# Holding back the third load of a row-gradient kernel until its first store is issued

## The chip, the cores and the metric

The kernel runs on one core of one Trainium2 chip. Its time is the device time of one execution in microseconds (us). A profile is one further execution, recorded by the hardware profiler; its span runs from the first to the last instruction, and its own device time is a little longer than its span.

## The reference

The input is an 8192 x 8192 array of float32, 268.4 MB. The output has the same size and is the gradient along each row:

```python
def reference(x: np.ndarray) -> np.ndarray:
    return np.gradient(x, axis=1)
```

Inside a row each output is half the difference of the right and the left neighbour. The first output of a row is the second element minus the first, the last one is the last element minus the one before it. There is one subtraction and one product for each element, and all 268.4 MB have to be read and 268.4 MB written: 536.9 MB through the core's 16 DMA engines.

## The kernel before

The rows are cut into 32 sets (`nsets`) of 256 rows. Each of the 128 partitions takes two whole rows (`R = 2`), which is 16384 elements, so a set is a tile of 128 x 16384 float32, 8.39 MB. Three buffers in SBUF, `slot0` to `slot2` (`NB = 3`), hold the sets in turn: set i lives in slot i mod 3. A slot has 64 elements of room in front of the input (`SH = 64`), and the result is written over the input, shifted to the left by that room.

One set goes through these steps. The line numbers are those of the profile.

1. The load (line 66) is one DMA of 8.39 MB. It is issued from SyncE's queue, shown as SP and, among the DMA queues, as q1. The load of set i + 3 waits for the store of set i, because it reuses its slot. It is queued right after set i's own work (line 120).
2. GpSimd (POOL) computes the differences at the ends of each row into `ends` (line 77). This is the first reader of the load, and so its start marks the landing of the load.
3. VectorE (DVE) computes the inner differences, halved, in one custom instruction of 128 x 16382 elements (line 88).
4. DVE, or in 12 sets POOL, copies the row ends into the result (line 99).
5. In sets 1 to 29 TensorE (PE) does two matmuls of 128 x 512 on zeros, whose result nobody reads (line 107). They wait for step 4, and the store waits for them. They serve as a pause.
6. The store (line 112) is one DMA of 8.39 MB from ScalarE's queue, shown as ACT and, among the DMA queues, as q10. The last two sets store from SP's queue, and the last set is computed and stored in two halves.

The work is in program order on every engine; `tc.manual_schedule()` leaves the order as written, and `chain` and `follow` name the instructions that each step has to wait for. At the start the loads of sets 0, 1 and 2 are issued one after the other, without any wait (line 71). They are moved in this order, since they are on one queue. The store of set 0 has no pause before it (`if 0 < i < nsets - 2`, line 103).

A DMA of 8.39 MB is split over all 16 DMA engines. Its packets are 64 KB each, 8 for each engine. The profile counts 5040 packets on q1 and 4320 on q10, the small writes that signal completion among them.

Of the kernel before, what the change touches and what calls it, by code (L numbers as in the profile page):

```python
# [1 line left out]

# [4 lines left out]


@with_exitstack
def kernel(  # L10
    ctx: ExitStack,
    tc: tile.TileContext,
    x: bass.AP,
    out: bass.AP,
):

    nc = tc.nc
    P = nc.NUM_PARTITIONS
    n, m = x.shape
    R = 2
    NB = 3
    SH = 64  # L30
    W = R * m
    nsets = n // (P * R)
    f32 = x.dtype

    x_sets = x.rearrange("(s p t) m -> s p (t m)", p=P, t=R)
    out_sets = out.rearrange("(s p t) m -> s p (t m)", p=P, t=R)

    pool = ctx.enter_context(tc.tile_pool(name="pool", bufs=1))
    slots = [pool.tile([P, SH + W], f32, name=f"slot{k}", tag=f"slot{k}") for k in range(NB)]
    ends = pool.tile([P, nsets, R, 2], f32, name="ends", tag="ends")  # L40
    zeros = pool.tile([P, 512], f32, name="zeros", tag="zeros")
    psum = ctx.enter_context(tc.tile_pool(name="psum", bufs=1, space=bass.MemoryType.PSUM))
    unread = psum.tile([1, 512], f32, name="unread", tag="unread")
    loads, stores = [], [[] for _ in range(nsets)]
    in_front = {}

    def chain(i, ins, *needed):

        group, engine = f"slot{i % NB}", ins.ins.engine
        keep = [o.ins for o in needed]
        if in_front.get(engine, (None,))[0] == group:
            keep.append(in_front[engine][1])
        tc.declare_no_dep(ins.ins, group=group, keep=keep, reason="implied by the needed step")
        tc.add_to_no_dep_group(group, ins.ins)
        in_front[engine] = group, ins.ins
        return ins

    def follow(ins, needed, reason):  # L60
        edge = mybir.DependencyInfo(mybir.DependencyClass.Sync, mybir.DependencyReason.DATA)
        tc.add_manual_dep(ins.ins, needed.ins.name, edge, reason=reason)

    def load(i):
        b = slots[i % NB]
        ins = nc.sync.dma_start(out=b[:, SH : SH + W], in_=x_sets[i])  # L66
        loads.append(chain(i, ins, *(stores[i - NB] if i >= NB else [])))

    with tc.manual_schedule():
        nc.vector.memset(zeros[:], 0.0)  # L70
        for i in range(NB):
            load(i)
        for i in range(nsets):
            b = slots[i % NB]
            xin = b[:, SH : SH + W].rearrange("p (t m) -> p t m", m=m)

            ins = nc.gpsimd.tensor_sub(  # L77
                out=ends[:, i, :, :],
                in0=xin[:, :, 1 : m : m - 2],
                in1=xin[:, :, 0 : m - 1 : m - 2],  # L80
            )
            at = [chain(i, ins, loads[i])]
            last = i == nsets - 1
            nr = 1 if last else R
            for r in range(0, R, nr):
                c0, c1 = r * m + 1, (r + nr) * m - 1

                ins = nc.vector._custom_dve(  # L88
                    dve_ops.TENSOR_TENSOR_REDUCE_SUB_MAX,
                    out=b[:, c0:c1],  # L90
                    in0=b[:, SH + c0 + 1 : SH + c1 + 1],
                    in1=b[:, SH + c0 - 1 : SH + c1 - 1],
                    s0=0.0,
                    s1=0.5,
                )
                halved = chain(i, ins, *at)
                res = b[:, r * m : (r + nr) * m].rearrange("p (t m) -> p t m", m=m)
                placer = nc.gpsimd if i % 5 in (1, 3) and not last else nc.vector
                ins = placer.tensor_copy(out=res[:, :, 0 : m : m - 1], in_=ends[:, i, r : r + nr, :])  # L99
                placed = chain(i, ins, halved)  # L100
                queue = nc.scalar if i < nsets - 2 else nc.sync
                pause = None
                if 0 < i < nsets - 2:


                    for k in range(2):
                        pause = nc.tensor.matmul(  # L107
                            out=unread[:], lhsT=zeros[:, 0:1], rhs=zeros[:], start=True, stop=True
                        )
                        if k == 0:  # L110
                            follow(pause, placed, "after the tile is computed")
                ins = queue.dma_start(  # L112
                    out=out_sets[i, :, r * m : (r + nr) * m], in_=b[:, r * m : (r + nr) * m]
                )
                stores[i].append(chain(i, ins, placed))
                if pause:
                    follow(ins, pause, "after the pause")
                at = [halved]
            if i + NB < nsets:
                load(i + NB)  # L120


# [1 line left out]
_INS = ['x']  # L124
_OUTS = [((8192, 8192), 'float32')]


# [23 lines left out]
```

## Time and profile before

| | us |
|---|---|
| six executions | 1248.38, 1248.56, 1248.81, 1257.55, 1257.81, 1261.25 |
| their median | 1253.18 |
| the profiled execution's own time | 1262.37 |
| its span | 1259.4 |
| DVE busy | 555.3 (44% of the span) |
| PE busy | 102.2 (8%) |
| POOL busy | 8.9 (1%) |
| packets on q1 and q10, share of 16 engines' span | 52.5% and 46.6% |

The six executions fall into two groups, one at 1248.4 to 1248.8 us and one at 1257.6 to 1261.3 us, with nothing between them; the median lies in the gap. The profiled execution is 1.1 us above the highest of the six.

Times inside the profile are us from the start of the span. Engine rows of the page show the busy share in tenths for 40 slices of the span, 31.5 us each. A row of the timeline gives the start, the duration, the engine, the line and the operation; the bracket at its end gives how long the engine had been idle and what it had waited for. Rows that end in "x3" or "x5" merge several instructions, and their duration runs from the first start to the last end. A row of the windows gives a stretch, the busy time of each engine in it, the granted TensorE clock, and last the DMA engines' mean busy share and the GB/s of the packets that started in it.

### The profile page before, as it was taken

To read this page: it belongs to the slowest core of one execution; us is meant where nothing else is said; L and a number is where in the kernel's file an instruction comes from. 1 tells how busy PE (TensorE), PEld (TensorE's weight loads), DVE (VectorE), ACT (ScalarE), POOL (GpSimd) and SP (SyncE) were. 2 spreads that over 40 slices of the span, in tenths; PEclk is the share of its full clock that TensorE was granted. 3 is DMA by queue.
4 is the path that set the end of the run, shared out by engine and by line. 5 is a ranking of instruction groups with operands and counts; after the bars stand their busy time and mean duration, and the time that the engine had idled before them with its cause. 6 is when DMAs were issued, how large, how long until landed. Compare 5 with 4: busy or idle time off the path is not lost.

```text
span 1259.4 us, 501 instructions
## 1 busy us (share of the span) xinstructions
PE 102.2 (8%) x116; PEld 9.8 (1%) x116; DVE 555.3 (44%) x55; POOL 8.9 (1%) x48
## 2 busy tenths in 40 slices
PE   0001110111100111011110111101111001110000
PEld 0000000000000000000000000000000000000000
DVE  2841555235553245523555335553345532455343
POOL 0000000000000000000000000000000000000000
PEclk9999995555555555555555555555555555555555
DMA  9999999999999999999999999999999999999996
GB/s 406 427 433 433 431 433 433 431 435 435 435 439 433 441 433 439 431 433 431 433 433 423 416 433 433 433 433 431 431 406 431 439 427 433 418 414 433 433 433 275
DMA packets 9361, 536.89 MB, mean 426 GB/s; under 512 B 1040, under 2 KB 1040, under 8 KB 1040
## 3 DMA queue, kind: packets, MB, share of 16 engines
q1 hardware_dynamic: 5040, 285.21, 52.5%
q10 hardware_dynamic: 4320, 251.66, 46.6%
q8 instruction: 1, 0.02, 0.0%
HBM read 268.44 MB, written 268.44 MB: 426 GB/s over the span
## 4 chain that ended last, share of the span: by engine, by line
DMA 70%; DVE 14%; another core or an unknown queue 9%; issue 3%; PE 2%; POOL 0%; SPq 0%; POOLq 0%; ACTq 0%
DMA slot<-in_x_dram 36%; DMA out_dram<-slot 34%; DVE slot L88 14%; PE unread L107 2%; POOL ends L77 0%; DVE slot L99 0%; SPq L66 0%; POOL slot L99 0%; POOLq L146 0%; ACTq L112 0%
## 5 line engine op out<-in xcount | busy, mean ns | idle before, releaser
L88 DVE CUSTOM_DVE_ANT_0 slot<-slot 128x16382 f32<-128x16382 f32 (+1 forms) x33 | 551.3, 16707 | 680.7 <-POOL ends L77 680.7
L107 PE MATMUL unread<-zeros 128*1 128x512 f32 x116 | 102.2, 1035 | 1065.4 <-DVE slot L99 603.9
L107 PEld LDWEIGHTS unread<-zeros 128*1 128x1 f32 x116 | 9.8, 104 | 1156.0 <-DVE slot L99 633.1
L77 POOL TENSOR_TENSOR ends<-slot 128x4 f32<-128x4 f32 x32 | 6.4, 200 | 1002.9 <-DMA slot<-in_x_dram 1002.9
L99 DVE COPY slot<-ends 128x4 f32<-128x4 f32 (+1 forms) x21 | 3.6, 172 | 0.7
L99 POOL COPY slot<-ends 128x4 f32<-128x4 f32 x12 | 2.3, 192 | 207.9 <-DVE slot L88 207.9
L70 DVE MEMSET zeros<- 128x512 f32 x1 | 0.5, 485 | 0.9 <-PEq L135 0.9
L135 POOL MEMSET const-bfloat16-1.0<- 128x1 bf16 x1 | 0.1, 103 | 0.0
L135 POOL MEMSET const-uint8-127<- 128x1 uint8 x1 | 0.1, 103 | 0.0
L135 POOL MEMSET const-float32-0.0<- 128x1 f32 x1 | 0.1, 99 | 0.2 <-issue 0.2
L135 POOL MEMSET const-float32-1.0<- 128x1 f32 x1 | 0.1, 99 | 0.0
## 6 DMA issues: line engine op xcount, KB each, us to landing
out_dram<-slot SPq DMA_DIRECT2D x2, 4096.0 KB, 20.3
slot<-in_x_dram SPq DMA_DIRECT2D x32, 48.9
out_dram<-slot ACTq DMA_DIRECT2D x30, 47.6
out_dram<-slot SPq DMA_DIRECT2D x1, 35.9
```

The costliest lines, as they stand in the source:

```text
L70: nc.vector.memset(zeros[:], 0.0)
L77: ins = nc.gpsimd.tensor_sub(out=ends[:, i, :, :], in0=xin[:, :, 1 : m : m - 2], in1=xin[:, :, 0 : m - 1 : m - 2],)
L88: ins = nc.vector._custom_dve(dve_ops.TENSOR_TENSOR_REDUCE_SUB_MAX, out=b[:, c0:c1], in0=b[:, SH + c0 + 1 : SH + c1 + 1], in1=b[:, SH + c0 ...
L99: ins = placer.tensor_copy(out=res[:, :, 0 : m : m - 1], in_=ends[:, i, r : r + nr, :])
L107: pause = nc.tensor.matmul(out=unread[:], lhsT=zeros[:, 0:1], rhs=zeros[:], start=True, stop=True)
L135: nc = _bacc.Bacc("TRN2", target_bir_lowering=False, num_devices=1)
```

## The change

Four things are different. The loads of sets 0 and 1 alone are issued at the start. The load of set 2 is issued from SP after the pause of set 0, the same pause that the store of set 0 now waits for; so that store and that load are released together. The pause of set 0 is new and short: one matmul of 128 columns. And ACT's queue, which the stores use, begins with a load of 16 x 16 elements into a small tile `few` that nobody reads.

```diff
     zeros = pool.tile([P, 512], f32, name="zeros", tag="zeros")
+    few = pool.tile([16, 16], f32, name="few", tag="few")
...
         nc.vector.memset(zeros[:], 0.0)
-        for i in range(NB):
-            load(i)
+
+        nc.scalar.dma_start(out=few[:], in_=x[0:16, 0:16])
+        load(0)
+        load(1)
         for i in range(nsets):
...
                 pause = None
-                if 0 < i < nsets - 2:
+                if i < nsets - 2:


-                    for k in range(2):
+                    for k in range(2 if i else 1):
+                        c = 512 if i else 128
                         pause = nc.tensor.matmul(
-                            out=unread[:], lhsT=zeros[:, 0:1], rhs=zeros[:], start=True, stop=True
+                            out=unread[:, 0:c], lhsT=zeros[:, 0:1], rhs=zeros[:, 0:c], start=True, stop=True
                         )
                         if k == 0:
                             follow(pause, placed, "after the tile is computed")
...
                 stores[i].append(chain(i, ins, placed))
                 if pause:
                     follow(ins, pause, "after the pause")
+                if i == 0:
+
+
+                    load(2)
+                    follow(loads[2], pause, "after the second load")
                 at = [halved]
             if i + NB < nsets:
                 load(i + NB)
```

## The prediction

> **What bounds the kernel now.** I read the engines' shares first: DVE 44%, PE 8%, POOL 1%. No compute engine bounds it. Then the slices and the queues:
>
> ```profile
> DMA  9999999999999999999999999999999999999996
> GB/s 406 427 433 433 431 433 433 431 435 435 435 439 433 441 433 439 431 433 431 433 433 423 416 433 433 433 433 431 431 406 431 439 427 433 418 414 433 433 433 275
> ...
> q1 hardware_dynamic: 5040, 285.21, 52.5%
> q10 hardware_dynamic: 4320, 251.66, 46.6%
> ```
>
> The DMA engines are busy in every slice but the last; the two queues fill 99.1% of the span. So 1259.4 us hold some 1249 us of packets on each engine. The trace's list of packets says how many that should be: 536.87 MB are 512 packets of 64 KB for each engine, and an undisturbed one starts 2.414 us after the one before: 512 x 2.414 = 1236.0 us. The rest is loss, and the windows show two kinds:
>
> ```profile
> 200.00:400.00 200.00, 17.26 (x20) 1.69 (x20) 87.84 (x9) 1.58 (x8) 0.53 1.00 435
> ...
> 800.00:1000.00 200.00, 17.11 (x20) 1.69 (x20) 90.37 (x9) 1.39 (x7) 0.53 1.00 428
> ...
> 1240.00:1250.00 10.00, 0.00 (x0) 0.00 (x0) 0.00 (x0) 0.00 (x0) 0.50 0.86 370
> 1250.00:1259.40 9.40, 0.00 (x0) 0.00 (x0) 0.00 (x0) 0.00 (x0) 0.50 0.05 21
> ```
>
> First, a share of 0.05 over the last 9.4 us is one engine of sixteen (1/16 = 0.06): by the packets fifteen engines end at 1249.2 to 1249.4 and one at 1258.1. **One engine lags**, and the end waits for it. Second, 435 GB/s at 200 to 400 us become 428 later at the same busy share: packets got longer. In the packets all this comes together. The laggard lands 0.5 us after the median engine in the load of set 1, 1.3 in the load of set 2, 3.8 in the store of set 1, then about 4.5 in stores until 460 us, and 12 to 15 from 615 us on. Every load waits for a store's last engine, so with a lag of 12 both queues run dry on the other fifteen, and from 660 us on the first packet of nearly every store takes 2.6 to 3.5 us on all engines instead of 2.418. That lengthening sums to 6.6 us per engine. The two groups of times, 1248.5 and 1257.6 to 1261.3, are 9 to 13 us apart, about what the tail's 9 and these 6.6 make together. I read them as "lag stays near 4" and "lag runs away"; that is an inference, for only one execution has a trace.
>
> **The change part by part.** The start:
>
> ```profile
> 0.74 118.42 SPq L66 DMA_DIRECT2D slot<-in_x_dram  x5
> ...
> 40.42 0.17 DVE L99 COPY slot<-ends 128x4 f32<-128x4 f32 x1
> 40.62 61.26 ACTq L112 DMA_DIRECT2D out_dram<-slot  x3
> 42.23 0.20 POOL L77 TENSOR_TENSOR ends<-slot 128x4 f32<-128x4 f32 x1 [19.11 <-DMA slot<-in_x_dram]
> ...
> 60.00 3.57 PE L107 MATMUL unread<-zeros 128*1 128x512 f32 x4 [60.00 <-POOL slot L99]
> ```
>
> *The short pause.* Two matmuls of 512 columns take 3.57 us; one of 128 columns is an eighth of that, 0.45, and I allow 0.6 with the handover. So the store of set 0 is issued at about 41.2 instead of 40.62. On ACT nothing is late behind it, the next store goes at 63.67. On the path it costs nothing: in before that store's first packet ran only at 46.8 to 47.7, behind packets of load 2. If that cover goes, it is the 0.6.
>
> *The third load.* Its issue moves on SP from 1.64 to about 41.2. Behind it on SP stands only the load of set 3, which waited until 82.59 for the store of set 0 anyway. Today its packets follow those of load 1 without a gap at 41.0 to 41.8. Afterwards the engines run out there and wait. Issue to first packet is, by the first load, 0.74 to 1.76 at the earliest engine and 2.70 at the latest: 1.0 to 2.0 us. So first packets come at 42.2 to 43.2 while load 1 ends at 41.4 in the median (41.8 at the last): about 1.1 us idle, between 0.3 and 2.8. The first packets at 1.8 took 3.1 us, 0.7 too long; I charge that again. What goes is a dent of the same kind:
>
> ```profile
> 42.00:44.00 2.00, 0.00 (x0) 0.00 (x0) 1.53 (x1) 0.20 (x1) 1.00 1.38 426
> 44.00:46.00 2.00, 0.00 (x0) 0.00 (x0) 2.00 (x1) 0.00 (x0) 1.00 0.30 98
> 46.00:48.00 2.00, 0.00 (x0) 0.00 (x0) 2.00 (x1) 0.00 (x0) 1.00 1.21 524
> ```
>
> Between 44 and 46 hardly a packet starts, because those running when the store's work arrived took 3.36 us in the mean, 0.94 too long. Sum: 1.1 + 0.7 - 0.9 = **+0.9 us**; bounds: 0.3 with no lengthening and the dent gone, -0.6; 2.8 with 0.7 and the dent kept by the second queue, +3.5.
>
> *The small load.* The trace has no DMA of this size. Nearest rows: a DMA's issue holds its queue 0.33 to 0.42 us, so if it delays load 0 by that it costs +0.4; if it takes a first-use cost off the store queue, that cost is at most the 0.94 dent, of which nothing is left to gain where I have counted it. Range -0.7 (the lengthening I charged above) to +0.4; I take +0.2, half an issue, since ACT issues it and SP the load.
>
> *After that.* Load 2 and store 0 share the engines from 42.6: 16 packets each engine, to about 82, where before load 2 landed at 80.2 and store 0 at 82.57. Load 3 is then issued at 82 to 83 (was 82.59), store 1 is queued already. The compute on set 2 starts 2 us later, and store 2 still comes far ahead of the end of store 1 at 115. So the order of the transfers stays, and the sum is +0.9 + 0.2 = **+1.1 us**: 1263.5 for the profiled execution, 1249.6 for the lower group, 1258.7 to 1262.4 for the upper.
>
> [...]
>
> **Forecast.** The lag begins where store 0 joins load 2 on engines that are mid-packet: the laggard, 0.7 us late, takes its turns in another order from 70 us on and is a packet pair behind at 118. With both queues released at once onto empty engines I expect that pair not to open, and the executions to fall in the lower group: **1249.6 us**, bounds 1248.5 - 0.6 - 0.7 = 1247.2 and 1248.5 + 3.5 + 0.4 = 1252.4. Chance 0.48.
>
> **Rivals.**
> - *The lag is not made at the join.* For: the laggard also has packets of 2.5 to 2.9 us at 55, 60, 65 and 126 us that no other engine has, and its growth from 4.5 to 12 comes at 460 to 615, far from the start. Then the mixture stays: median 1253.2 + 1.1 = 1254.3, chance 0.14; or the new start makes the upper group the usual one: 1258 to 1263, middle 1260.5, chance 0.27.
> - *The stores run dry from the start* (slower). A store is issued 21.2 us after its load lands (242.9 to 264.1), and in the good stretch that is 5.6 us before the store ahead of it ends (269.7). A lag in loads 5 us above the 2.2 there uses this up. If the new order of turns brings that in the first sets, the 14 stores with 6.6 us of lengthening become all 30: 6.6 x 16/14 = 7.5 more on the top of the upper group: 1262.4 + 1.1 + 7.5 = 1271. Against: the order after 82 us is that of before. Chance 0.09.
> - *The engines are not idle when the load is issued.* 41.2 is before load 1's end at 41.4 to 41.8. With a first packet under 0.5 us after issue, nothing empties, the idle term falls to 0 and the time is 1248.5. That is inside the forecast's bounds and counted there.
> - *Faster by over 1%* (below 1240.6) would need less than 1236.0 + 1.9 (start) + 2.97 (outside the span) = 1240.9. Only a price I misread allows it: 0.02.
>
> **How the numbers follow.** A measurement of this kernel can tell about 1% from no change. Within 1% (1240.6 to 1265.7): 0.48 + 0.14 + 0.27 = 0.89. The range runs from the lower bound 1247 to 1262, which leaves out the slow rival, the 0.02 and some 0.08 of the upper group: 0.81 inside.
>
> **What would show it.** In the changed profile: no packet starts for about a microsecond near 42; load 2 and store 0 land together at 81 to 84; the lag of the last engine stays under 5 us, with 433 GB/s or more in the stretches after 600 us; the stretch with a share near 0.05 at the end shrinks from 9 us to 2 or 3. Wrong would be a lag of 10 us or more again, or first packets of stores near 3 us from the first sets on.

## The result and the profile after

The changed kernel takes 1260.6 us in the median of 34 executions (1255.7 to 1269.8); the kernel before takes 1253.3 us in the median of 69 (1245.8 to 1262.2). The ratio is 1.0064, with a 95% interval of 1.0047 to 1.0081: **about 8 us slower**, between 5.9 and 10.2. The forecast was 1249.6 us, a gain of some 4; the time went the other way. Both kernels spread over 14 to 16 us; the whole spread has moved up, its lower end by 9.9 us and its upper end by 7.7. The two groups of the first six executions of the kernel before are not there in 69: 41 of these lie between 1248.9 and 1257.5 us, where the six had left a gap.

The profiled execution of the changed kernel took 1258.76 us, with a span of 1256.4. The slices of its page, 31.4 us each, show where the time went:

```profile
DMA  9999999999999999999999999999999999999997
GB/s 403 384 365 413 434 434 434 434 436 434 434 430 434 434 434 434 434 434 434 434 436 434 434 434 434 434 434 434 432 434 434 434 434 434 434 434 434 434 434 340
```

From the fifth slice on, the rate is 434 GB/s almost without a break, steadier than before. The second, third and fourth slices have 384, 365 and 413. Against 434 that is (50 + 69 + 21) / 434 x 31.4 = 10.1 us of lost transfer between 31 and 126 us. The same three slices of the kernel before, 427, 433 and 433, lose 0.7. The engines were busy almost throughout: the packets were slow, not absent. (By the list of packets an engine stood without one for 1.3 us near 42 us, and for 0.8 us in all between 50 and 100.) The windows of the changed kernel narrow it down (columns as before; the last two are the DMA share and the GB/s of packets started in the stretch):

```profile
40.00:42.00 2.00, 0.59 (x2) 0.09 (x2) 0.68 (x2) 0.00 (x0) 1.00 0.00 0
42.00:44.00 2.00, 0.00 (x0) 0.00 (x0) 1.36 (x1) 0.20 (x1) 1.00 1.84 524
44.00:46.00 2.00, 0.00 (x0) 0.00 (x0) 2.00 (x1) 0.00 (x0) 1.00 0.09 33
...
42.00:97.00 55.00, 3.57 (x4) 0.34 (x4) 20.70 (x2) 0.59 (x3) 0.73 1.00 377
97.00:152.00 55.00, 3.57 (x4) 0.34 (x4) 26.67 (x3) 0.20 (x1) 0.53 0.99 421
1240.00:1250.00 10.00, 0.00 (x0) 0.00 (x0) 0.00 (x0) 0.00 (x0) 0.50 0.94 406
1250.00:1256.40 6.40, 0.00 (x0) 0.00 (x0) 0.00 (x0) 0.00 (x0) 0.50 0.17 72
```

No packet starts between 40 and 42, the idle gap that the prediction looked for. The dent at 44 to 46 is still there. The last row, a share of 0.17 over 6.4 us, is more than one late engine: by the packets the sixteen engines end at 1248.5 to 1255.0, spread over the whole 6.5 us, where before fifteen ended within 0.2 us and one 8.8 us later. What was not expected is the row 42 to 97: 377 GB/s at a busy share of 1.00. The kernel before moved 419 in that stretch and 437 in the next:

```profile
42.00:97.00 55.00, 3.57 (x4) 0.34 (x4) 33.78 (x2) 0.59 (x3) 1.00 0.99 419
97.00:152.00 55.00, 7.14 (x8) 0.68 (x8) 18.07 (x3) 0.39 (x2) 1.00 1.01 437
```

The timeline of the changed kernel shows the two issues, and the landing of load 2 as the start of POOL's work on set 2:

```profile
40.77 0.59 PE L111 MATMUL unread<-zeros 128*1 128x128 f32 x2 [40.77 <-DVE slot L102]
41.39 0.33 SPq L67 DMA_DIRECT2D slot<-in_x_dram  x1
41.39 0.37 ACTq L116 DMA_DIRECT2D out_dram<-slot  x1
...
93.29 0.20 POOL L80 TENSOR_TENSOR ends<-slot 128x4 f32<-128x4 f32 x1 [33.17 <-DMA slot<-in_x_dram]
93.42 0.33 SPq L67 DMA_DIRECT2D slot<-in_x_dram  x1
```

Load 2 and store 0 are issued at the same instant, 41.39, and land together, the load at 93.2 and the store at 93.4; the issue of load 3 at 93.42 follows the latter. Before they had landed at 80.1 and 82.6; the row of the kernel before for the landing of load 2 is

```profile
80.21 0.20 POOL L77 TENSOR_TENSOR ends<-slot 128x4 f32<-128x4 f32 x1 [20.27 <-DMA slot<-in_x_dram]
```

In the list of packets, load packets that started between 47 and 85 us took 3.05 us in the mean and store packets 2.62, where 2.418 is the undisturbed value. From 101 us on they are at 2.418 again. The sum of everything above 2.418 in the stretch 48 to 105 us is 7.1 us for each engine in the mean; before it was 0.04. Of the 7.1, 5.7 fall before 95 us, where the two transfers share the engines, and 1.3 at 95 to 101, where load 3 joins. The engines do not lose the same: load 2 lands on the first of them at 87.3 and on the last at 93.2.

### The profile page after: what moved, and what is told of

Its sections match the earlier page's. It is cut to its first block, busy times and chain, and to the rows that moved or that the text cites. A ratio compares the mean times of both kernels' runs of the same rounds, so it can differ in the third digit from the quotient of the medians.

```text
span 1256.4 us, 507 instructions
## 1 busy us (share of the span) xinstructions
PE 102.8 (8%) x118; PEld 9.9 (1%) x118; DVE 555.3 (44%) x55; POOL 8.8 (1%) x48
## 4 chain that ended last, share of the span: by engine, by line
DMA 73%; DVE 15%; another core or an unknown queue 4%; issue 3%; PE 3%; POOL 0%; SPq 0%; POOLq 0%; ACTq 0%
DMA slot<-in_x_dram 39%; DMA out_dram<-slot 34%; DVE slot L91 15%; PE unread L111 3%; POOL ends L80 0%; DVE slot L102 0%; POOL slot L102 0%; SPq L67 0%; POOLq L155 0%; ACTq L116 0%
## 5 line engine op out<-in xcount | busy, mean ns | idle before, releaser
L111 PE MATMUL unread<-zeros 128*1 128x512 f32 (+1 forms) x118 | 102.8, 1025 | 1063.1 <-DVE slot L102 650.2
```

Source lines behind the costliest of these rows:

```text
L111: pause = nc.tensor.matmul(out=unread[:, 0:c], lhsT=zeros[:, 0:1], rhs=zeros[:, 0:c], start=True, stop=True)
```

## The experiments

In all of them the question is when load 2 and store 0 are issued, and how fast their packets are. A rate below 390 GB/s in the window from 42 to 97 us marks the slow stretch; the clean kernels have 409 or more. The theories were: *released together* (two transfers that start at the same time on empty engines slow each other until they are done), *same place* (they work through the same packet index, hence addresses or partitions in step), *small load* (the early load on the store queue), and *hold-back alone*. Six of the kernels have a single execution, the profiled one (shifted rows, split store, the leads of 0.42 and 1.7 us for the store and of 0.43 us for the load, and half of the compute); the kernel with the lead of 0.42 us for the store was run again, twelve times. For the others the ratio is to the kernel before, timed beside them.

### Store first by 3.6 us, and load first by 3.6 us

```diff
                 if i == 0:
+                    for k in range(2):
+                        later = nc.tensor.matmul(
+                            out=unread[:], lhsT=zeros[:, 0:1], rhs=zeros[:], start=True, stop=True
+                        )
                     load(2)
-                    follow(loads[2], pause, "after the second load")
+                    follow(loads[2], later, "after the longer pause")
```

> Load 2 waits for two more matmuls of 512 columns after the short pause (about 3.6 us), so store 0 has the engines alone first. In the changed kernel load 2 and store 0 were both released at 41.4 us and both landed at 93.3, with their packets at 3.2 and 2.6 us in the mean instead of 2.418. Same-place theory (load and store work through the same packet index, so through addresses in step, at the same time): the head start of one to two packets removes it; packets at 2.42, store 0 lands at 82 or before, load 2 at about 86, time 5 to 8 us below the changed kernel. Released-together theory (two transfers that start at the same instant on empty engines): the same as here, since they no longer start together. Small-load theory (the early load on the store queue changes that queue): nothing changes, both land at 93 or later.

The second kernel puts the two extra matmuls between the load and the store instead, so that load 2 goes first.

> The reverse: load 2 goes after the short pause, store 0 waits for two more matmuls of 512 columns (about 3.6 us). This is nearest to the kernel before, where store 0 joined a running load 2. Same-place and released-together theories: packets at 2.42, load 2 lands at about 80, store 0 at about 84, time 5 to 8 us below the changed kernel, 1 to 2 us above the kernel before. Small-load theory: both still land at 93 or later.

Window of the kernel with the store first, then of the one with the load first:

```profile
42.00:97.00 55.00, 5.45 (x7) 0.47 (x5) 25.34 (x2) 0.59 (x3) 0.57 1.00 417
```

```profile
42.00:97.00 55.00, 6.09 (x8) 0.55 (x7) 34.62 (x3) 0.55 (x3) 0.72 0.99 417
```

Both are at 417. (The 3.2 us that the expectation gives for load packets of the changed kernel is 3.13 over all 128 packets of load 2.) Store packets are at 2.418, and so are the load's after its first. The landings are 88.6 (load) and 78.8 (store) in the one, 78.9 and 83.7 in the other. Times: ratio 1.0037 (1.0001 to 1.0072) with the store first, 1.0009 (0.9977 to 1.0042) with the load first. The slow stretch is gone either way, which fits both main theories and speaks against the small load, present in both. By its ratio the kernel with the store first kept a loss of 4.6 us, with an interval of 0.1 to 9.0; its profile has other losses later on (6.8 us of lengthening after 105 us, a last engine 7.6 us late).

### Without the small load

```diff
-        nc.scalar.dma_start(out=few[:], in_=x[0:16, 0:16])
         load(0)
```

> The changed kernel without the small early load on the store queue. Small-load theory: packets of load 2 and store 0 at 2.42 us, both land at about 82, time 5 to 8 us below the changed kernel. Same-place and released-together theories: load 2 and store 0 land at 93 as in the changed kernel, time as there within 1 us.

```profile
42.00:97.00 55.00, 3.57 (x4) 0.34 (x4) 22.20 (x2) 0.50 (x3) 1.00 0.98 375
```

375 GB/s, landings at 91.7 and 91.9, ratio 1.0112 (1.0052 to 1.0172, four executions from 1256.2 to 1270.6). The interval covers the 1.0064 of the changed kernel; four executions cannot tell the two apart. The small load is not the cause of the slow stretch.

### Other rows for load 2, and a split store

```diff
-        ins = nc.sync.dma_start(out=b[:, SH : SH + W], in_=x_sets[i])
+        src = x_sets[i]
+        if i == 2:
+            src = x[2 * P * R + 8 : 3 * P * R + 8, :].rearrange("(p t) m -> p (t m)", t=R)
+        ins = nc.sync.dma_start(out=b[:, SH : SH + W], in_=src)
```

> The changed kernel, but load 2 reads the rows 8 further on in HBM, four packets (256 KB) away from the place in step with store 0; its partitions in SBUF stay the same. The output of that one set is that of the shifted rows, the amount of work is the same. Same-place theory with the place in HBM: packets at 2.42 us, both transfers land at about 82. Same place in SBUF, or released together, or the small load: both land at 93 as in the changed kernel.

```diff
-                ins = queue.dma_start(
-                    out=out_sets[i, :, r * m : (r + nr) * m], in_=b[:, r * m : (r + nr) * m]
-                )
-                stores[i].append(chain(i, ins, placed))
+                for p0, p1 in ((0, 16), (16, P)) if i == 0 else ((0, P),):
+                    ins = queue.dma_start(
+                        out=out_sets[i, p0:p1, r * m : (r + nr) * m], in_=b[p0:p1, r * m : (r + nr) * m]
+                    )
+                    stores[i].append(chain(i, ins, placed))
...
```

> The changed kernel, with store 0 cut into two DMAs on the same queue, partitions 0 to 15 and then 16 to 127: one packet for each engine and then seven. Load 2 is one DMA as before, so an engine that works on the n-th packet of each no longer touches the same partition of SBUF. Same-partition theory: packets at 2.42 us, load 2 and store 0 land at about 82. Released-together theory: both still land at 88 to 94 with loads at 2.7 to 3.4 us a packet.

Window with the shifted rows, then with the split store:

```profile
42.00:97.00 55.00, 3.57 (x4) 0.34 (x4) 22.05 (x2) 0.58 (x3) 1.00 1.01 385
```

```profile
42.00:97.00 55.00, 3.57 (x4) 0.34 (x4) 23.45 (x2) 0.58 (x3) 1.00 0.99 356
```

Both are slow. With shifted rows the two land at 91.9 and 92.1. With the split store the load lands at 90.5, the second part of the store at 95.0, and the mean load packet is 2.59 us, under the 2.7 to 3.4 expected of the released-together theory. The shift of 256 KB changes nothing, so the same place in HBM is not the cause, as far as one shift can tell. For the same partition in SBUF the answer is mixed. The split store shows the disturbance at its largest in one packet: the first store packet of every engine took 7.7 to 8.6 us. After it the loss is about half of that of the changed kernel, 2.7 us per engine instead of 5.7 between 48 and 95 us, and two of the sixteen engines lose no more than 0.1. That partitions in step have a part in the slow packets is therefore not ruled out.

### How much stagger is needed

One more matmul before load 2, of 128 columns:

```diff
+                    later = nc.tensor.matmul(
+                        out=unread[:, 0:128], lhsT=zeros[:, 0:1], rhs=zeros[:, 0:128], start=True, stop=True
+                    )
                     load(2)
-                    follow(loads[2], pause, "after the second load")
+                    follow(loads[2], later, "after the longer pause")
```

> The changed kernel with load 2 released one more matmul of 128 columns later than store 0, about 0.45 us. Released-together theory: what counts is that the store's packets run before the load's work arrives; the first packet came 1.0 us after the issue, so 0.45 us is too little and both land at 88 to 94. Theory of an instant collision of the two issues alone: gone, both land at 82 to 84.

The same edit with 512 columns:

> The same with one more matmul of 512 columns, about 1.8 us. Released-together theory: store packets run for 0.8 us when the load's issue comes, so it is as with 3.6 us: store 0 lands at 79 to 82, load 2 at 84 to 88, packets at 2.42 us but for the first of the load. If it takes a whole packet ahead (2.4 us after a first packet at 1.0): still 88 to 94.

And the mirror, with load 2 after the short pause and store 0 one matmul of 128 columns later:

> The mirror of the small stagger: load 2 after the short pause, store 0 one matmul of 128 columns later, about 0.42 us. If any small difference between the two issues is enough, whichever is first: packets at 2.42 us after the first two or three, load 2 lands at 79 to 83, store 0 at 82 to 85. If it has to be the store that is ahead: both land at 88 to 94.

Timeline and windows of the kernel with the store 0.42 us ahead, in two fences:

```profile
40.98 0.37 ACTq L116 DMA_DIRECT2D out_dram<-slot  x1
41.40 0.33 SPq L67 DMA_DIRECT2D slot<-in_x_dram  x1
...
86.02 0.20 POOL L80 TENSOR_TENSOR ends<-slot 128x4 f32<-128x4 f32 x1 [26.33 <-DMA slot<-in_x_dram]
```

```profile
42.00:97.00 55.00, 3.57 (x4) 0.34 (x4) 27.97 (x2) 0.57 (x3) 1.00 0.98 409
```

The window of the mirror, with the load 0.43 us ahead (41.06 and 41.49):

```profile
42.00:97.00 55.00, 3.57 (x4) 0.34 (x4) 33.16 (x2) 0.59 (x3) 1.00 1.01 425
```

A stagger of 0.42 us is enough, in either order. With the store ahead it is the first packets alone that suffer (2.2 us per engine between 39 and 48 us), and from 48 to 105 us the lengthening is 0.08. The load lands at 85.9, the store at 81.1, and not both at 88 to 94 as I had written for the released-together theory. In the mirror they land at 80.8 and 83.2, as written for any small difference between the issues. With 1.7 us of stagger (issues at 40.99 and 42.70) the load lands at 88.4 and the store at 80.5, the store as expected and the load just beyond its range. My own bound, that the leading transfer's packets must already run, missed: in the 0.42 case the load was issued at 41.40 and the first store packet started at 41.86. A lead of one *issue* over the other is enough.

The lists of packets show what such a lead changes. In the three slow profiles with the whole store (changed, without the small load, shifted rows) load and store packets alternate one for one from the first, for five packets or more on every one of the 16 engines (the packets followed from the end of one to the start of the next). In every clean profile each engine has two or more packets of the transfer that leads before the first of the other, so that the packets of the two with the same number do not follow each other. These runs do not tell whether it is the common start or the packets in step that makes them slow: apart from the split store, no run has one without the other.

The staggered kernel was also timed:

> Load 2 released one matmul of 128 columns after store 0, 0.42 us later in the trace; in one look the slow stretch was gone. If the slow stretch is all that the change costs beside its idle microsecond: the time goes down to that of the kernel before plus 0 to 2 us (ratio 1.000 to 1.002). If holding the load back costs more than that later (a larger lag): ratio 1.004 or more. If the start on empty engines keeps the lag small, as the prediction had it: ratio 0.997 or less.

```profile
42.00:97.00 55.00, 3.49 (x4) 0.34 (x4) 28.04 (x2) 0.59 (x3) 0.72 0.99 412
```

Median 1250.6 us of 12 (1249.7 to 1256.6), ratio 1.0006 (0.9985 to 1.0026). This is the first of the three outcomes written down. The slow stretch, and what it does to the engines later, is therefore all that can be told from noise of what the change costs; the interval leaves room from -1.9 to +3.3 us. A gain is not seen either.

### Released together while load 1 still runs

```diff
+                if i == 0:
+                    c1 = m - 1
                 ins = nc.vector._custom_dve(
```

> The changed kernel with the inner differences of set 0 computed for the first row of each partition only (8190 elements instead of 16382), so that half of that set's output is not written with results. Store 0 and load 2 are released together at about 32.8 us, while load 1 still runs until 42. Idle-engines theory (two transfers released together are slow only where the engines have nothing to do): packets at 2.42 us but for one dent, load 2 and store 0 land at 79 to 83. If the common release alone is enough: load 2 and store 0 with packets of 2.7 to 3.4 us, landing at 88 or later.

Timeline of the two issues and of the landing of load 1, and the window of the 55 us that follow the issues:

```profile
32.40 0.33 SPq L67 DMA_DIRECT2D slot<-in_x_dram  x1
32.40 0.37 ACTq L118 DMA_DIRECT2D out_dram<-slot  x1
50.61 0.20 POOL L80 TENSOR_TENSOR ends<-slot 128x4 f32<-128x4 f32 x1 [27.82 <-DMA slot<-in_x_dram]
```

```profile
32.00:87.00 55.00, 3.94 (x6) 0.34 (x4) 17.22 (x1) 0.39 (x2) 1.00 0.99 419
```

The issues coincide to 0.01 us, and yet store packets are at 2.418 and load packets at 2.422 in the mean; there is the one dent at the start. So the common release is not enough. The landings were not at the 79 to 83 I had written. Load 1 shares the engines with store 0 from 37 us and lands at 50.5, store 0 at 74.7, load 2 at 89.4. Load 2 stands behind load 1 on its queue: its first packet runs at 51.9 us, 14.5 us after the first of store 0 at 37.4. The two issues coincide, but the two transfers do not start together, so the run does not show that idle engines are what it takes; it fits packets in step as well. This run's 1267.1 us come from elsewhere: 14.1 us of lengthening after 105 us and a last engine 8.7 us late.

### Load 2 back at the start, and no pauses at all

```diff
         load(1)
+        load(2)
...
-                if i == 0:
-                    load(2)
-                    follow(loads[2], pause, "after the second load")
```

> The changed kernel with load 2 back at the start; the small load and the short pause before store 0 stay. If the hold-back alone makes the loss: packets of load 2 and store 0 at 2.42 us but for one dent, both land at 79 to 83 as in the kernel before, and the time is within 2 us of it. If the small load or the short pause carries part of the loss: 2 to 8 us above it.

```profile
42.00:97.00 55.00, 3.88 (x5) 0.43 (x6) 34.62 (x3) 0.49 (x3) 1.00 0.98 419
```

Load packets and store packets at 2.418, landings 78.9 and 81.4, ratio 0.9996 (0.9969 to 1.0022). The small load and the short pause cost nothing that can be told from noise (-3.9 to +2.8 us); the hold-back carries the loss.

The last one asks about the lag, in the kernel before:

```diff
-                if 0 < i < nsets - 2:
+                if False:
```

> The kernel before without its pauses: every store is issued 3.6 us earlier. If the upper group comes from stores issued after the store ahead of them has ended on most engines: 3.6 us more reserve removes most of the first packets of 2.6 to 3.5 us, and the time lies at 1246 to 1250 us. If the pause is what keeps the lag from growing: the time rises to 1258 us or more.

Ratio 1.0004 (0.9973 to 1.0035); ten executions from 1247.7 to 1262.2. Neither expectation holds: 3.6 us of reserve do not remove the high times, and the pauses do not prevent them.

### All profiles side by side

Per engine, from the lists of packets, in us. The kernel with half of the compute is left out, since its transfers meet at 37 us. "Idle" is the gap near 42; "first" is the lengthening above 2.418 between 39 and 48 us, "slow" between 48 and 105, "later" after 105. The next column is the mean load packet started between 47 and 85. "Lag" is how far the last engine ends behind the median one.

| kernel | idle | first | slow | load packet | load 2, store 0 land | later | lag | time |
|---|---|---|---|---|---|---|---|---|
| before | 0.0 | 0.9 | 0.0 | 2.43 | 80.1, 82.6 | 8.5 | 8.8 | 1262.4 |
| changed | 1.3 | 1.4 | 7.1 | 3.05 | 93.2, 93.4 | 0.8 | 4.9 | 1258.8 |
| no small load | 0.8 | 1.3 | 6.5 | 2.98 | 91.7, 91.9 | 0.0 | 2.8 | 1256.2 |
| shifted rows | 0.9 | 1.4 | 6.6 | 3.00 | 91.9, 92.1 | 8.1 | 7.3 | 1265.2 |
| split store | 0.9 | 6.7 | 3.7 | 2.59 | 90.5, 95.0 | 0.2 | 3.9 | 1258.9 |
| store first, 3.6 us | 0.7 | 0.8 | 1.4 | 2.58 | 88.6, 78.8 | 6.8 | 7.6 | 1259.2 |
| store first, 0.42 us | 0.6 | 2.2 | 0.1 | 2.59 | 85.9, 81.1 | 1.0 | 4.0 | 1249.9 |
| store first, 0.42 us, timed | 0.7 | 2.1 | 0.0 | 2.58 | 85.9, 81.0 | 1.5 | 3.1 | 1250.6 |
| store first, 1.7 us | 0.6 | 1.0 | 1.2 | 2.59 | 88.4, 80.5 | 1.5 | 2.2 | 1249.4 |
| load first, 3.6 us | 0.9 | 1.8 | 0.1 | 2.64 | 78.9, 83.7 | 0.7 | 1.4 | 1247.7 |
| load first, 0.43 us | 0.9 | 1.7 | 0.0 | 2.42 | 80.8, 83.2 | 2.1 | 8.7 | 1258.0 |
| load 2 at the start | 0.0 | 0.9 | 0.0 | 2.42 | 78.9, 81.4 | 0.8 | 5.8 | 1249.9 |
| no pauses | 0.0 | 0.9 | 0.0 | 2.42 | 79.1, 81.5 | 0.7 | 4.7 | 1248.2 |

The mean load packet of a staggered kernel holds its one slow first packet; the column "slow" is the better mark. Subtracting idle, first, slow, later and lag from the time leaves 1240.9 to 1244.8 us in every row. The columns therefore account for the times to about 2 us either way, and a single time says nothing of the change without them: the mirror is clean at the start and still took 1258.0, by its lag of 8.7. The lag is not one thing in all rows: in the kernel before and in the mirror it is one engine behind fifteen that end within 0.2 us, in the changed kernel it is the end of a spread that begins in the slow stretch.

## Why the prediction was wrong

**What bounds the kernel: right, but for the groups.** DMA engines that hardly pause and two kinds of loss, long packets and a late last engine, account for the table above. The two groups of times were a chance of six executions: most of the 69 lie between them. A forecast of "the lower group" therefore had no such group to fall into.

**The idle term: right.** Put at 1.1 us, between 0.3 and 2.8; it measured 1.3. The first packet came 0.96 us after the issue (41.39 to 42.35), against 1.0 from the start of the kernel. The rival by which the engines would not be idle at all is gone. The Trainium skill, "DMA: Bandwidth & Descriptors", section "Anatomy of one DMA — SWDGE (gpsimd) path", puts the fixed cost of a DMA on the path of GpSimd at about 2.0 us, most of it the wait until the last byte is confirmed as landed. That is no price for this gap, which lies between an issue on the queues of SP and ACT and the first packet; the trace decides, with 0.96 us. The short pause was priced right as well: 0.6 us, and 0.62 from its start to the two issues (40.77 to 41.39).

**The first packets: under-sized.** 0.7 was charged and 0.9 credited for the old dent; 1.4 was measured where 0.7 was charged.

**The step that failed** is "Load 2 and store 0 share the engines from 42.6: 16 packets each engine, to about 82". It took every packet after the first at 2.418 us, because the kernel before shows that value whenever loads and stores alternate. But in every such place one of the two was already running when the other was issued. Sharing from a common start on idle engines stood nowhere in that trace, and I gave it no range. It measured 93.4 instead of 82 and 7.1 us of lengthening that is in no term. With it the sum is 1.3 (idle) + 1.4 - 0.9 (first packets) + 7.1 = 8.9 instead of 1.1 us, or 9.7 with the 0.8 us of idle time between 50 and 100, beside 8 us in the times with an interval of 5.9 to 10.2. The store first by 0.42 us takes the 7.1 to 0.1 and the time back to that of the kernel before, which shows that this step cost the time. The Trainium skill, "DMA: Bandwidth & Descriptors", section "Issuing engines are not separate DMA queues", says that transfers issued by different engines run on the same 16 DMA engines and interleave. The packets do alternate here, but at 3.05 and 2.62 us; plain interleaving would have given the 82.

**The forecast's group: wrong.** I expected the lag not to open after a start on empty engines. In the changed profile it did not run away as before: the stores' last engine was 8.5 us behind the median at 131 us, settled at 6 to 7.5, and ended 4.9 late, and from 600 us on the rate is 433 to 435 GB/s. But it did open, by the slow stretch itself, and one profile of 1258.8 us says nothing of the executions near 1269; the 34 spread over 14 us as before. The rival "the lag is not made at the join, the mixture stays" comes nearest: 1254.3 + 7.1 = 1261.4, beside a median of 1260.6. That the rival by which the upper group becomes the usual one names 1260.5 is luck, and so is the upper end of the range, 1262, which was set for that group: the lowest times moved as well, from 1245.8 to 1255.7, and the lag of the changed profile, 4.9, is not the 8.8 of the profile of before.

**The slower rival: not met.** It priced stores that run dry from the first sets at 1271. In the changed profile the lengthening after 105 us is 0.8 us, against 8.5 before.

**What stays open.** Why a common start on idle engines slows the packets for the whole of both transfers, and why a lead of 0.42 us prevents it, is not shown; that neither queue then gets work prepared ahead of the other is only an idea, and so is a collision of packets that stay in step. A run that puts the two transfers one packet out of step and still starts them together, with no split of the store, would tell more. Leads between 0.01 and 0.42 us were not tried. Nor is it known what makes one engine late, or why its lag runs away in some executions: the run without pauses argues against the account I gave.

## What to carry to other kernels

Where the trace shows a load and a store released together onto DMA engines that have run empty, try to issue one of them some 0.4 us ahead, or to keep a transfer in flight across the join; either took the slow stretch away here, with transfers of 8.39 MB, and no other size was tried. When a step is moved to a moment with other neighbours, look whether the trace of before shows that combination at all; if it doesn't, the price per packet is unknown and needs a range of its own. In a kernel bound by DMA, compare GB/s at a busy share of 1.00: "always busy" hides slow packets.

## What was not expected of the hardware

- Two 8.39 MB transfers, a load and a store, issued at the same instant on idle DMA engines took 52 us to land (41.4 to 93.4) instead of the 38 to 46 us that each took with a lead of 0.42 to 3.6 us for either, and all four profiles with that start were slow (landings at 90.5 to 95.0). With 0.42 us between the issues, or with another load still in flight, the packets ran at 2.418 us after the first ones.
- With the store cut into 16 and 112 partitions, its first packet took 7.7 to 8.6 us on each of the 16 engines.
- The kernel with load 2 first by 3.6 us showed the smallest loss of all profiles: 1247.7 us, of which 1.4 us are lag. It is the lowest of its ten executions; their median is 1254.5.
